# Tiny products in the left-out arms of an expert layer, an activation moved ahead, and a sum spread between blocks

## Chip, cores and metric

One core of a Trainium2 chip runs the whole kernel. The metric is the device time of one execution in microseconds (us), lower is better.

## What is computed

The reference is an encoder of two layers on 256 tokens of 1024 features. Each layer has a mixer of four branches and a feed-forward part; that of the first layer is dense, that of the second sends each token to two of eight experts. The change touches the experts alone:

```python
def moe_swiglu(x, router, w1, w3, w2):
    logits = jnp.einsum('bsd,de->bse', x, router)
    top_logit, top_idx = lax.top_k(logits, 2)
    top_w = jax.nn.softmax(top_logit, axis=-1)
    gate = jnp.sum(jax.nn.one_hot(top_idx, 8) * top_w[..., None], axis=-2)
    out = jnp.zeros_like(x)
    for e in range(8):                       # w1, w3: 1024 x 3584, w2: 3584 x 1024
        out = out + gate[..., e:e+1] * ((silu(x @ w1[e]) * (x @ w3[e])) @ w2[e])
    return out
```

All arithmetic of the experts is float32, and each expert has 42 MiB of weights.

## The kernel before

**Weights.** They come from HBM in blocks of 1 MiB (`fetch`, line 118, on SP's DMA queue), 42 for an expert: blocks 0 to 27 hold w1 and w3, 28 to 41 hold w2. They land in a ring of 21 places, and a block's load waits until the block 21 before it has been used.

**Bins.** An expert's tokens (`gather`, line 759, puts them into `xe`) stand in four bins of 32. A product takes one bin as its 32 stationary columns and streams 512 columns of weights; four such products, one for each fourth of TensorE's columns, lie beside each other in one bank of PSUM. In the profile a float32 product is two MATMUL records, so a bin of one block is 8 records. How many bins an expert needs is known only on the chip. It is loaded into TensorE's registers (`sel`), and every further bin stands in a `tc.If` (line 841) that TensorE's sequencer branches on; the other engines have no part in it.

**Stages of an expert.** `firsts(x_, q)` (line 972) runs quads q = 0, 1, 2 of eight blocks each: `quad` multiplies bin 0, then, nested, bins 1 to 3 (lines 855 to 866). Quad 3 has four blocks and takes the bins in pairs: bins 0 and 1 always, bins 2 and 3 under one `If`. `second` (line 924) does the same by pairs for the 14 blocks of w2. After a quad come `act` (silu on ScalarE, line 885, times the other half on VectorE, line 886, which reads and frees the quad's PSUM banks), `turn` (eight transposes, line 895), `turned` (copies by ScalarE and VectorE, lines 905 and 903). `where` (line 943) transposes the tokens' places. `evacuate` (hilo, lines 163 and 164) copies an expert's result out of PSUM, and `add` (lines 965 and 969) multiplies it back to the tokens, for each half t of them, with eight products on TensorE and two operations on VectorE.

**The left-out arm.** The first block of a quad must leave zeros in the banks of bins that are left out, so there the `If` has an `Else` with products of zeros, 128 stationary by 512 streamed columns in bfloat16, one for each bank (lines 858 to 860, 929). All other blocks have an `If` without an `Else`.

**Order.** Inside `tc.manual_schedule()` the order of the program is the order of each engine. An expert's w2 blocks 12 and 13 are put off until after the next expert's first quad:

```python
                        firsts(x_, 0)
                    if last:
                        seconds(last, (12, 13))
                        last.evacuate()
                    ...
                    x_.act(0)
                    ...
                    firsts(x_, 1)
                    x_.turn_places(0)
                    x_.turn(0)
                    x_.turned(0)
                    x_.act(1)
                    if last:
                        last.add()
                    x_.second_places()
                    firsts(x_, 2)
```

PSUM has four banks for the quads (`mm`), two for the second products (`s`) and two for transposes and sums (`tr`). So `firsts(x_, 1)` waits for `act(0)` to free the quad's banks, and `add`, `turn` and `where` share the two of `tr`.

Of the kernel before, what the change touches and what calls it, by code (L numbers as in the profile page):

```python
# [71 lines left out]
def trunk(tc, A, out):  # L72
    nc = tc.nc
# [573 lines left out]
    def moe(xs, gb):  # L647
        with tc.tile_pool(name="moe", bufs=1, reuse_waits="tile") as ep:
# [48 lines left out]
            zero = ep.tile([128, 512], BF16, name="zero")  # L697
# [46 lines left out]
            def places_of(e, off, oh=None, ts=(0, 1)):  # L744

                oh = ep.tile([128, 2, 128], F32, name="oh", bufs=2) if oh is None else oh
                for t in ts:
                    nc.vector.tensor_scalar(oh[:, t], iota, off + 1.0, pos[:, t, e:e + 1], op0=ALU.add, op1=ALU.is_equal)
                return oh

            def gather(oh):

                xe = ep.tile([128, 8, 128], F32, name="xe", bufs=2)
                for j in range(2):
                    ps = trp.tile([128, 4, 128], F32, name="tr")
                    for i in range(4):
                        k = 4 * j + i
                        for t in range(2):
                            nc.tensor.matmul(ps[:, i], x[t][:, k * 128:(k + 1) * 128], oh[:, t], start=t == 0, stop=t == 1)
                    if j:  # L760
                        nc.scalar.activation(xe[:, 4:8], ps, AF.Copy)
                    else:
                        nc.vector.tensor_copy(xe[:, 0:4], ps)
                return xe
# [54 lines left out]
            _, sel = nc.values_load_multi_w_load_instructions(armi[0:1, 0:NE], engines=[PE], min_val=0, max_val=3)  # L819
            over = nc.values_load(mosti[0:1, 0:1], min_val=0, max_val=S)  # L820

            class Expert:


# [9 lines left out]
                        else:  # L834
                            self.w[n] = block(self.e, n)

                def bins_over(self, n, some, none=None):

                    if self.inner:
                        return some()  # L840
                    with tc.If(sel[self.e] > n - 1) as c:  # L841
                        some()
                    if none:
                        with c.Else():
                            none()

                def quad_places(self, q):
                    self.ps[q] = [mm.tile([128, 512], F32, name="mm") for _ in range(4 if q < 3 else 2)]
# [1 line left out]
                def quad(self, q, u):  # L850

                    w, ps = self.w[8 * q + u], self.ps[q]

                    def product(k, r, g, bank, c0):
                        nc.tensor.matmul(ps[bank][32 * g:32 * g + 32], self.xe[:, k, 32 * r:32 * r + 32], w[:, c0:c0 + 512],  # L855
                                         start=k == 0, stop=k == 7)

                    def zeros(r):
                        for i in range(r, len(ps)):
                            nc.tensor.matmul(ps[i], zero[:, 0:128], zero, start=True, stop=True)  # L860

                    def bin_(r):
                        for c in range(4):
                            product(u, r, c, r, c * 512)
                        if r < 3:
                            self.bins_over(r + 1, lambda: bin_(r + 1), (lambda: zeros(r + 1)) if u == 0 else None)

                    def pair(m):
                        for kk in range(2):
                            for rr in range(2):  # L870
                                for c in range(2):
                                    product(2 * u + kk, 2 * m + rr, 2 * rr + c, m, kk * 1024 + c * 512)

                    if q < 3:
                        bin_(0)
                    else:
                        pair(0)
                        self.bins_over(2, lambda: pair(1), (lambda: zeros(1)) if u == 0 else None)

                def act(self, q):  # L880

# [29 lines left out]
                def second(self, j):  # L911

                    w, q, c = self.w[28 + j], j // 4, j % 4

                    def pair(m):
                        for i in range(2):
                            for half in range(2):
                                for rr in range(2):
                                    g = 2 * half + rr
                                    if q < 3:  # L920
                                        h = self.h[q][m][:, rr, i, 32 * c:32 * c + 32]
                                    else:
                                        h = self.h[q][0][:, m, i, 32 * (2 * rr + c):32 * (2 * rr + c) + 32]
                                    nc.tensor.matmul(self.py[m][32 * g:32 * g + 32], h,  # L924
                                                     w[:, i * D + half * 512:i * D + half * 512 + 512],
                                                     start=j == 0 and i == 0, stop=j == 13 and i == 1)

                    def zeros():
                        nc.tensor.matmul(self.py[1], zero[:, 0:128], zero, start=True, stop=True)

                    pair(0)
                    self.bins_over(2, lambda: pair(1), zeros if j == 0 else None)

                def where_places(self):
                    self.wtr = trp.tile([128, 2, 2, 128], F32, name="tr")
# [33 lines left out]
                            nc.vector.scalar_tensor_tensor(acc[t][:, c], ps[h], gate[:, t, self.e:self.e + 1], acc[t][:, c],  # L969
                                                           op0=ALU.mult, op1=ALU.add, accum_out=sums[:, t, h:h + 1])  # L970

            def firsts(x_, q):
                x_.quad_places(q)
                for u in range(8 if q < 3 else 4):
                    x_.blocks(8 * q + u)
                    x_.quad(q, u)

            def seconds(x_, js):
                for j in js:
                    x_.blocks(28 + j)  # L980
                    x_.second(j)

            with tc.manual_schedule():
                last = None
                for e in range(NE + 1):
                    x_ = None
                    if e < NE:
                        x_ = Expert(e, oh, xe)
                        firsts(x_, 0)
                    if last:  # L990
                        seconds(last, (12, 13))
                        last.evacuate()
                    if e == NE:
                        break
                    x_.act(0)
                    if e + 1 < NE:
                        oh = places_of(e + 1, 0)
                    firsts(x_, 1)
                    x_.turn_places(0)
                    x_.turn(0)  # L1000
                    x_.turned(0)
                    x_.act(1)
                    if last:
                        last.add()
                    x_.second_places()
                    firsts(x_, 2)
                    x_.turn_places(1)
                    x_.turn(1)
                    x_.turned(1)
                    x_.act(2)  # L1010
                    seconds(x_, range(4))
                    if e + 1 < NE:
                        xe = gather(oh)
                    firsts(x_, 3)
                    x_.turn_places(2)
                    x_.turn(2)
                    x_.turned(2)
                    x_.act(3)
                    seconds(x_, range(4, 8))
                    x_.turn_places(3)  # L1020
                    x_.turn(3)
                    x_.turned(3)
                    x_.where_places()
                    x_.where()
                    x_.wheres()
                    seconds(x_, range(8, 12))
                    if e == NE - 1:
                        gt = gb()
                    last = x_
                last.add(0)  # L1030

                with tc.If(over > CAP):
                    for e in range(NE):
                        oh = places_of(e, CAP)
                        x_ = Expert(e, oh, gather(oh), inner=True)
                        x_.where_places()
                        x_.where()
                        x_.wheres()
                        x_.second_places()
                        for q in range(4):  # L1040
                            firsts(x_, q)
                            x_.act(q)
                            x_.turn_places(q)
                            x_.turn(q)
                            x_.turned(q)
                            seconds(x_, range(4 * q, min(4 * q + 4, 14)))
                        x_.evacuate()
                        x_.add()
            with tc.manual_schedule():
# [6 lines left out]
                for t in range(2):  # L1056
                    for h in range(2):
                        c = norms[t].finish(h)
# [11 lines left out]
    for l in range(DEPTH):  # L1070
        xs = mixer(l, xs, lambda l=l: load_gb(1 + 2 * l))
        if l % 2 == 0:
            xs = ffn(xs, lambda: load_gb(2))
    moe(xs, lambda: load_gb(4))
    ctx.close()

# [145 lines left out]
```

## Time and profile before

| | |
|---|---|
| median of 3 runs | 1717.95 us (1715.56 to 1719.6) |
| profiled execution | 1715.06 us |
| its span in the trace | 1713.0 us |
| TensorE busy | 1580.6 us, 92% of the span |
| VectorE, ScalarE busy | 572.5 us, 426.5 us |
| experts, first product to last | 672.6 to 1695 us of the span |
| weights in the experts' part | 310 MB at up to 419 GB/s |

In the trace PE is TensorE's products, PEld its weight loads, PEq its sequencer. A timeline's row merges neighbouring records of one line: start, length, engine, line, operation, and how many; in brackets stand the idle time before it and what ended it. A length runs to the modelled end of the last record, and the next product of a stream begins a little before that, so periods are taken from start to start.

### The profile page before, as it was taken

How to read it: one execution, taken by the hardware profiler on the slowest of the kernel's cores; microseconds unless marked ns; L12 is line 12 of the kernel's file. 1: busy time of each engine (PE TensorE's matmuls, PEld its weight loads, DVE VectorE, ACT ScalarE, POOL GpSimd, SP SyncE). 2: the span in 40 equal slices, each digit the busy share in tenths (PEclk: the TensorE clock that was granted, in tenths of full speed). 3: DMA queues.
4: the chain of work that ended last, by engine and by line, in shares of the span. 5: the costliest groups of instructions: out<-in, count | busy, mean ns of one | idle time of the engine just before them, and what ended most of it. 6: DMA issues, size and time to landing. Idle time of an engine off the chain costs nothing. (4 is left out here: it accounts for less than half of the span.)

```text
span 1713.0 us, 26968 instructions
## 1 busy us (share of the span) xinstructions
PE 1580.6 (92%) x11305; PEld 820.9 (48%) x11322; DVE 572.5 (33%) x1070; ACT 426.5 (25%) x704; POOL 28.7 (2%) x29
## 2 busy tenths in 40 slices
PE   8999999999999998898899998899898899898896
PEld 7687878888868785131333332232232232232232
DVE  7688685554769674001001000100100100100102
ACT  4556644443565662010100000000010000100001
POOL 1000000000100000000000000000000000000000
PEclk9999999999999999999999999999999999999998
DMA  8345545555555547999999888778899778999700
GB/s 349 126 148 178 194 167 204 176 193 177 184 188 173 221 169 289 419 419 418 420 419 390 297 288 311 284 258 342 318 408 380 258 286 304 420 419 413 301 12 27
DMA packets 66975, 468.91 MB, mean 274 GB/s; under 512 B 7552, under 2 KB 8192, under 8 KB 11264
## 3 DMA queue, kind: packets, MB, share of 16 engines
q1 hardware_dynamic: 66816, 466.55, 71.3%
q8 instruction: 129, 2.11, 0.5%
q14 instruction: 30, 0.25, 0.0%
HBM read 465.48 MB, written 1.05 MB: 272 GB/s over the span
## 5 line engine op out<-in xcount | busy, mean ns | idle before, releaser
L855 PE MATMUL mm<-raw,xe 128*32 128x512 f32 x4416 | 519.6, 601 | 74.4 <-PEq L841 53.3
L855 PEld LDWEIGHTS mm<-raw,xe 128*32 128x32 f32 x4416 | 133.4, 110 | 430.3 <-issue 411.9
L924 PE MATMUL s<-raw,eh 128*32 128x512 f32 x2688 | 305.9, 594 | 11.5 <-PEq L841 8.7
L171 PE MATMUL mm<-w,xh 128*128 128x512 f32 (+2 forms) x1184 | 313.5, 385 | 1.9 <-ACT xh L163 1.9
L139 DVE TENSOR_TENSOR w<-raw,w 128x1024 fp32r<-128x1024 f32 (+1 forms) x198 | 238.4, 1208 | 135.2 <-ACT w L135 134.4
L135 ACT ACTIVATE w<-raw 128x1024 fp32r<-128x1024 f32 (+1 forms) x198 | 206.3, 1047 | 198.4 <-PE mm L171 172.7
L171 PEld LDWEIGHTS mm<-w,xh 128*128 128x128 f32 x1184 | 215.6, 189 | 45.5 <-ACT xh L163 3.6
L924 PEld LDWEIGHTS s<-raw,eh 128*32 128x32 f32 x2688 | 85.7, 109 | 209.4 <-issue 201.9
L171 PE MATMUL mm<-w,xl 128*128 128x512 f32 (+2 forms) x592 | 178.1, 384 | 0.7 <-DVE xl L164 0.7
L903 DVE COPY eh<-tr 128x512 f32<-128x512 f32 x24 | 16.6, 692 | 453.9 <-PE tr L895 453.9
L905 ACT ACTIVATE eh<-tr 128x512 f32<-128x512 f32 x32 | 19.1, 597 | 565.9 <-PE tr L895 565.9
L164 DVE TENSOR_TENSOR ey<-s,ey 128x512 fp32r<-128x512 f32 x16 | 10.7, 689 | 374.0 <-ACT ey L163 374.0
L171 PEld LDWEIGHTS mm<-w,xl 128*128 128x128 f32 x592 | 108.0, 189 | 22.2 <-issue 1.5
L163 ACT ACTIVATE ey<-s 128x512 fp32r<-128x512 f32 x16 | 9.1, 596 | 273.1 <-PE s L924 158.2
L520 DVE SCALAR_TENSOR_TENSOR ac<-ud,smc,ac 128x256 f32<-128x256 f32 x120 | 53.2, 479 | 0.7
L171 PE MATMUL mm<-xh,w 128*128 128x256 f32 x256 | 45.2, 289 | 0.0
L886 DVE TENSOR_TENSOR fs<-mm,fs 128x256 f32<-128x256 f32 x112 | 39.9, 415 | 15.2 <-ACT fs L885 15.1
L171 PE MATMUL mm<-w,hh 128*128 128x512 f32 x144 | 44.4, 389 | 0.0
L965 PE MATMUL tr<-ey,ohT 64*128 64x512 f32 x128 | 29.5, 480 | 13.6 <-DVE acc L969 6.7
L895 PEld LDWEIGHTS tr<-ident,fs 128*128 128x128 f32 x224 | 24.0, 141 | 34.7 <-issue 33.2
L171 PEld LDWEIGHTS mm<-xh,w 128*128 128x128 f32 x256 | 36.3, 191 | 3.2 <-issue 3.0
L885 ACT ACTIVATE fs<-mm 128x256 f32<-128x256 f32 x112 | 34.4, 399 | 13.0 <-PE mm L855 13.0
(200 smaller groups left out, 1021.0 us busy)
## 6 DMA issues: line engine op xcount, KB each, us to landing
raw<-wmoe SPq DMA_DIRECT2D x334, 1024.0 KB, 9.0
raw<-wpre SPq DMA_DIRECT2D x95, 1024.0 KB, 4.9
gb<-lnp SPq DMA_DIRECT2D x5, 1024.0 KB, 6.5
raw<-wpre SPq DMA_DIRECT2D x4, 704.0 KB, 5.9
z<-biasB SPq DMA_DIRECT2D x8, 256.0 KB, 2.7
raw<-wmoe SPq DMA_DIRECT2D x4, 512.0 KB, 7.9
z<-cw SPq DMA_DIRECT2D x2, 640.0 KB, 6.5
x<-x SPq DMA_DIRECT2D x2, 512.0 KB, 4.0
```

What stands on the lines that cost most here:

```text
L135: nc.scalar.activation(self.w[h][0], raw[:, h * self.n:(h + 1) * self.n], AF.Copy)
L139: (eng or nc.vector).tensor_tensor(wl, raw[:, h * self.n:(h + 1) * self.n], f(wh), op=ALU.subtract)
L171: nc.tensor.matmul(ps, o[i], o[j], start=start and q == 0 and k == 0, stop=stop and q == 2 and k == n - 1)
L520: later.append(lambda c=c, k=k, w=w: nc.vector.scalar_tensor_tensor(ac[:, c], ud[:, c, k:k + S], w(k), ac[:, c], op0=ALU.mult, op1=ALU.add))
L855: nc.tensor.matmul(ps[bank][32 * g:32 * g + 32], self.xe[:, k, 32 * r:32 * r + 32], w[:, c0:c0 + 512], start=k == 0, stop=k == 7)
L885: nc.scalar.activation(s, ps[:, 0:256], AF.Silu)
L886: nc.vector.tensor_tensor(s, ps[:, 256:512], s, op=ALU.mult)
L895: nc.tensor.transpose(self.tr[q][r // 2][:, r % 2, i], s[:, i * 128:(i + 1) * 128], ident)
L903: nc.vector.tensor_copy(h, tr)
L905: nc.scalar.activation(h, tr, AF.Copy)
L924: nc.tensor.matmul(self.py[m][32 * g:32 * g + 32], h, w[:, i * D + half * 512:i * D + half * 512 + 512], start=j == 0 and i == 0, stop=j = ...
L965: nc.tensor.matmul(ps[h], self.ohT[r, m, t], self.y[r, i, m], start=m == 0 and i == 0, stop=m == 1 and i == 1)
```

## The change

Three things. An `Else` arm now stands in every skip: where it held nothing, it holds `mark`, one bfloat16 product of zeros with 32 stationary columns and one streamed column, into the first bank that is left out (which holds zeros). `act(0)` of an expert stands ahead of the last expert's blocks 12 and 13 and of its `evacuate`. And `last.add()` is no longer after the second quad: its two halves stand behind blocks 3 and 6 of that quad.

```diff
+            def mark(ps):
+                nc.tensor.matmul(ps[0:32, 0:1], zero[:, 0:32], zero[:, 0:1], start=True, stop=True)
...
-                def bins_over(self, n, some, none=None):
+                def bins_over(self, n, some, none):
                     if self.inner:
                         return some()
                     with tc.If(sel[self.e] > n - 1) as c:
                         some()
-                    if none:
-                        with c.Else():
-                            none()
+                    with c.Else():
+                        none()
...
                     def zeros(r):
-                        for i in range(r, len(ps)):
-                            nc.tensor.matmul(ps[i], zero[:, 0:128], zero, start=True, stop=True)
+                        if u:
+                            mark(ps[r])
+                        else:
+                            for i in range(r, len(ps)):
+                                nc.tensor.matmul(ps[i], zero[:, 0:128], zero, start=True, stop=True)
...
-                            self.bins_over(r + 1, lambda: bin_(r + 1), (lambda: zeros(r + 1)) if u == 0 else None)
+                            self.bins_over(r + 1, lambda: bin_(r + 1), lambda: zeros(r + 1))
...
-                        self.bins_over(2, lambda: pair(1), (lambda: zeros(1)) if u == 0 else None)
+                        self.bins_over(2, lambda: pair(1), lambda: zeros(1))
...
                     def zeros():
-                        nc.tensor.matmul(self.py[1], zero[:, 0:128], zero, start=True, stop=True)
+                        if j:
+                            mark(self.py[1])
+                        else:
+                            nc.tensor.matmul(self.py[1], zero[:, 0:128], zero, start=True, stop=True)
                     pair(0)
-                    self.bins_over(2, lambda: pair(1), zeros if j == 0 else None)
+                    self.bins_over(2, lambda: pair(1), zeros)
...
-            def firsts(x_, q):
+            def firsts(x_, q, between={}):
                 x_.quad_places(q)
                 for u in range(8 if q < 3 else 4):
                     x_.blocks(8 * q + u)
                     x_.quad(q, u)
+                    if u in between:
+                        between[u]()
...
                         firsts(x_, 0)
+                        x_.act(0)
                     if last:
                         seconds(last, (12, 13))
                         last.evacuate()
                     if e == NE:
                         break
-                    x_.act(0)
                     if e + 1 < NE:
                         oh = places_of(e + 1, 0)
-                    firsts(x_, 1)
+                    firsts(x_, 1, {u: lambda t=t: last.add(t) for t, u in enumerate((3, 6))} if last else {})
                     x_.turn_places(0)
                     x_.turn(0)
                     x_.turned(0)
                     x_.act(1)
-                    if last:
-                        last.add()
                     x_.second_places()
```

## Rows read from the trace of the kernel before

**Rows 1.** Page, part 5: xcount | busy, mean ns | idle before, releasers.

```profile
L855 PE MATMUL mm<-raw,xe 128*32 128x512 f32 x4416 | 519.6, 601 | 74.4 <-PEq L841 53.3
```

**Rows 2.** Instructions of line 841: engine, operation, count, duration ns, first, last.

```profile
L841 PEldq EVENT_SEMAPHORE  x211: 51/51/51, 677.0 to 1627.9; - x106
```

**Rows 3.** DMA issues of three stretches, then busy times of one (last: GB/s).

```profile
raw<-wmoe SPq DMA_DIRECT2D x18, 1024.0 KB, 5.2
...
raw<-wmoe SPq DMA_DIRECT2D x79, 1024.0 KB, 17.0
...
raw<-wmoe SPq DMA_DIRECT2D x294, 1024.0 KB, 9.4
...
672.60:864.40 191.80, 164.24 (x1338) 50.12 (x1343) 21.07 (x57) 21.46 (x48) 0.00 (x0) 0.99 1.01 419
```

**Rows 4.** TensorE's timeline, expert 3, third quad, three bins a block.

```profile
1087.89 2.78 PE L855 MATMUL mm<-raw,xe 128*32 128x512 f32 x24
1090.93 2.78 PE L855 MATMUL mm<-raw,xe 128*32 128x512 f32 x24 [0.25 <-issue]
1094.16 2.78 PE L855 MATMUL mm<-raw,xe 128*32 128x512 f32 x24 [0.45 <-PEq L841]
```

**Rows 5.** TensorE's timeline, expert 0, first quad, two bins a block.

```profile
672.63 1.92 PE L855 MATMUL mm<-raw,xe 128*32 128x512 f32 x16
...
675.02 1.92 PE L855 MATMUL mm<-raw,xe 128*32 128x512 f32 x16
677.41 1.92 PE L855 MATMUL mm<-raw,xe 128*32 128x512 f32 x16 [0.46 <-PEq L841]
```

**Rows 6.** TensorE's timeline, expert 1, first quad, one bin a block.

```profile
773.80 1.06 PE L855 MATMUL mm<-raw,xe 128*32 128x512 f32 x8 [0.17 <-PEq L841]
...
775.55 1.06 PE L855 MATMUL mm<-raw,xe 128*32 128x512 f32 x8
...
778.03 1.06 PE L855 MATMUL mm<-raw,xe 128*32 128x512 f32 x8 [0.17 <-PEq L841]
```

**Rows 7.** TensorE's timeline, expert 0, second products, one pair a block.

```profile
735.85 1.92 PE L924 MATMUL s<-raw,eh 128*32 128x512 f32 x16 [0.25 <-issue]
...
740.05 1.93 PE L924 MATMUL s<-raw,eh 128*32 128x512 f32 x16 [0.17 <-PEq L841]
```

**Rows 8.** TensorE's timeline, expert 2, second quad, four bins, eight blocks.

```profile
898.34 27.67 PE L855 MATMUL mm<-raw,xe 128*32 128x512 f32 x256 [2.47 <-DVE fs L886]
```

**Rows 9.** TensorE's timeline, expert 0, places' transposes, then second products.

```profile
764.55 1.08 PE L943 MATMUL tr<-ident,oh 128*32 128x128 f32 x32
765.44 1.90 PE L924 MATMUL s<-raw,eh 128*32 128x512 f32 x16
```

**Rows 10.** Weight loads (PEld) in time, expert 3, third quad.

```profile
1088.78 0.13 PEld L855 LDWEIGHTS mm<-raw,xe 128*32 128x32 f32 x4 [0.30 <-issue]
```

**Rows 11.** TensorE's waits, 672 to 1694 us; all engines' timeline, expert 5.

```profile
PE mm L855 <- DVE fs L886: 9.8, 4, 2.5
...
1322.94 1.41 DVE L886 TENSOR_TENSOR fs<-mm,fs 128x256 f32<-128x256 f32 x4
...
1323.45 4.48 PE L855 MATMUL mm<-raw,xe 128*32 128x512 f32 x24 [2.47 <-DVE fs L886]
```

**Rows 12.** TensorE's timeline, expert 3, after the second quad.

```profile
1082.23 1.09 PE L895 MATMUL tr<-ident,fs 128*128 128x128 f32 x8 [0.46 <-PEq L841]
...
1086.10 0.50 PE L965 MATMUL tr<-ey,ohT 64*128 64x512 f32 x1 [0.80 <-DVE acc L969]
1086.77 1.20 PE L965 MATMUL tr<-ey,ohT 64*128 64x512 f32 x7 [0.17 <-DVE acc L969]
```

**Rows 13.** TensorE's timeline, expert 0, after the second quad.

```profile
711.21 1.09 PE L895 MATMUL tr<-ident,fs 128*128 128x128 f32 x8 [0.46 <-PEq L841]
713.46 1.06 PE L855 MATMUL mm<-raw,xe 128*32 128x512 f32 x8 [1.16 <-issue]
```

**Rows 14.** Busy times of a stretch; last: clock, DMA share, GB/s.

```profile
1480.00:1500.00 20.00, 16.68 (x99) 4.55 (x99) 4.35 (x12) 1.70 (x5) 0.00 (x0) 0.83 1.01 418
```

## The prediction

> **What bounds the kernel now.** I read the page's groups first, then the instructions of the `If` line, TensorE's timeline expert by expert, and last the loads. TensorE's products at line 855 are the costliest group, and 53.3 of the 74.4 us of idle time ahead of them were ended by TensorE's own sequencer at line 841, the `If` [rows 1]. At that line the sequencer ran 211 semaphore instructions [rows 2]. The timeline gives each expert's bins by the records of one block (8 a bin): experts 0 to 7 have 2, 1, 4, 3, 2, 3, 1 and 3. An expert has 37 skips without an `Else` (21 blocks of quads 0 to 2, three of quad 3, 13 of w2). With one or two bins all 37 are left out, with three only the 21 innermost, with four none: 4 x 37 + 3 x 21 = 211. So the count is that of the empty left-out arms, and arms that hold zeros have none. An empty arm still has to count its products as done, and does it by an instruction that waits until TensorE's products have ended. The pipeline runs dry and starts anew; the reader is to see it as the bracket of idle time in every period.
>
> Are the weights late? 18 blocks were issued before the first expert product and 79 more until 864.4, where expert 2 begins; each took 17.0 us to land at 419 GB/s, so 2.50 us a block [rows 3]. 17.0 / 2.50 = 6.8 were still on the way, so 18 + 79 - 6.8 = 90 had landed, where TensorE had used 82 (42 of expert 0, 40 of expert 1). It was 7 to 8 blocks ahead, 18 to 20 us. At the start of expert 7 it was 18 + 294 - 7 - 292 = 13 blocks, 32 us [rows 3]. TensorE's order is the bound throughout; the weights are so only if it gains over some 19 us before 864.4.
>
> **Part 1, the marks.** Four bins with no skip run at 27.67 us for 256 records, 0.865 us a bin, 0.86 without the end of the last one [rows 8]. Against that:
> three bins, empty arm: 1094.16 - 1090.93 = 3.23, less 2.58, is 0.65 [rows 4]; two bins 2.39 less 1.72 is 0.67 [rows 5]; one bin 2.48 / 2 = 1.24 less 0.86 is 0.38 [rows 6]; a pair 4.20 / 2 = 2.10 less 1.72 is 0.38 [rows 7]. The nested ones cost more, which I put down to a jump to the block's end behind the wait. So 105 arms cost 0.66 and 106 cost 0.38 us, 109.6 us in all.
>
> What replaces it shows only by neighbours. An arm with one, two and three products of zeros has a period of 3.04, 2.39 and 1.75 us [rows 4 to 6], over the bins 0.46, 0.67 and 0.89: 0.215 us for each 512 streamed columns and 0.245 fixed. The fixed part has neither the semaphore's wait nor a visible jump, but those products are 128 columns wide and want all of the array. That is the upper end for a mark, whose one column streams in nothing: **0.245**. The lower end is a change between two kinds of products that both stand 32 wide: 16 transposes of places (32 records, a quarter of the columns, so 16 / 4 x 0.86 / 4 = 0.86 us) are followed by the next stage after 0.89 [rows 9], a switch of **0.03**. Below nothing can't be, as a product is added. I take **0.08**, near the lower end, since a mark has that shape; the rest is for the one weight load behind it that can't be made early.
>
> First the row: weight loads 32 columns wide start while the products of the half before are streaming (four loads at 1088.78, in a stretch whose products are never idle) [rows 10]. [...]
>
> Gain for a nested arm 0.66 - 0.08 = 0.58, for a direct one 0.30. Experts 2 to 7: 84 nested (63 + 21), 53 direct (16 + 37): 48.7 + 15.9 = **64.6 us**. Experts 0 and 1: 21 x 0.58 + 53 x 0.30 = 28.1 us, before the cap below.
>
> **Part 2, `act(0)` ahead.** Now ScalarE and VectorE take it up after `evacuate`, and TensorE stands before quad 1 until VectorE has freed the banks: four waits of 2.4 to 2.5 us, 9.8 in all [rows 11], and three of 1.81 that the trace names "issue" (experts 3, 4, 6). VectorE's share is 1.41 us after some 0.4 on ScalarE [rows 11], and blocks 12 and 13 give at least two pair periods, 4.2 us [rows 7], of cover. So the waits go; `evacuate` slips behind, and its first user, `add`, now comes four blocks later, over 3.6 us. Both queues hold nothing else there but the next places (VectorE). No DMA is moved, so SP's queue keeps its order. Gain 2.4 us in expert 1 and **12.8** in 2 to 7.
>
> **Part 3, the sums.** From `turn` to quad 2 it is 1087.89 - 1082.23 = 5.66 us [rows 4, 12]; the seven experts with a sum give 5.65 to 6.51, 41.7 in all, 35.5 of it in 2 to 7. Without a sum it is 713.46 - 711.21 = 2.25, in which 1.16 is the wait for `act(1)` [rows 13]. So the sums now cover a wait which comes back, and that is what is late next. A sum's half that waits for nothing takes about 1087.89 - 1086.77 = 1.12 us for seven of eight products and the way back [rows 4, 12], so 1.2; two of them in the quad cost 2.4. Nothing else wants the `tr` banks there; with one bin, block 7 is short and `turn` may wait 0.2 us for VectorE. Gain in 2 to 7: 35.5 - 6 x (2.25 + 2.4) = 7.6, I take **7.3**; 1.5 in expert 1.
>
> **Part 4, the clock.** [...] Without the stalls I take it to stay up: **4.7** us in experts 4 to 6, 1.0 in expert 1. From 0 to 4.7 is open.
>
> **The cap.** Experts 0 and 1 would gain 28.1 + 2.4 + 1.5 + 1.0 = 33 us, but the loads run at their full rate there and can't come earlier: 18 to 20, **19**. From expert 2 on the loads wait for places, so they move with TensorE; expert 6 gains 37 x 0.30 and some 5 more, 16 us, of 32 at hand.
>
> **Sum.** 19 + 64.6 + 12.8 + 7.3 + 4.7 = 108.4. The profiled execution took 1715.06 us (span 1713.0), so 1606.7; the median shown lies 2.9 above it, which gives **1610**.
>
> **The rivals.**
> A, the forecast: 1610, chance 0.68.
> B, the mark is as dear as the fixed part of a zeros' arm, 0.245 (its loads and the next ones bare): experts 2 to 7 give 84 x 0.415 + 53 x 0.135 = 42, and experts 0 and 1 still reach the cap (8.7 + 7.2 + 4.9 = 21). 19 + 42 + 24.8 = 86: 1632. The two kinds of zeros' arms speak for it, rows 9 and 10 against. Chance 0.20.
> C, the moved stages give nothing: another wait comes in, above all the one for `act(1)` [rows 13] grown by a sum's operations on VectorE, and the clock falls all the same. Marks and cap alone: 84 us, 1634. Against it speaks that VectorE is idle in the quads. Chance 0.06.
> D, it doesn't do what it says: the left-out arms keep their wait, and the mark comes on top. The moves' 24.8 + 4.9 less 211 x 0.08 leave 13 us: 1705. The arms with zeros, which have no semaphore instruction [rows 2], speak against. Chance 0.03.
> E, slower: each mark empties the array in both directions and holds up the sequencer, at the skips. The arms' 109.6 and 29.7 for the moves cover 139.3 / 211 = 0.66 us a mark; beyond that point the kernel is slower, and at 0.8 it is 1747. A whole product of zeros with 512 columns has 0.46 [rows 4]. Chance 0.03.
>
> **How the numbers follow.** With the mark at 0.03 the sum gains 7 us more, and short stalls of the sequencer in expert 6 may go too: 1592 at the low end. At the high end B with half of the moves' gain: 1655; D and E are left out, 0.06, and the outer parts of A to C. A difference under 0.2% (3.4 us) can't be told from none here. Faster holds A, B, C and most of D: 0.95; same 0.02; slower 0.03.
>
> **What would show it.** Line 841 has no semaphore instructions left; three, two and one bins have periods of about 2.66, 1.80 and 0.94 us, a pair 1.80; the 2.47 and 1.81 us waits are gone; quad 2 begins 2.25 us after `turn`, with a wait for `act(1)`; late in expert 1 TensorE waits for weights, and expert 2 begins near 845; the clock holds. I would be wrong by the mark's price (periods 0.17 longer), by weights that bind elsewhere, or by sums that stall inside the quad.

## The result: 1605.45 us, and the profile after

The changed kernel takes **1605.45 us** (median, 1603.25 to 1606.61) against 1717.74 beside it: a ratio of 0.9345 [0.9329, 0.9361]. 1610 was forecast, in a range of 1592 to 1655. The spans of the two profiled executions, 1713.0 and 1604.6 us, differ by 108.4 us.

Two groups of the page after (count | busy, mean ns | idle time before them and what ended it):

```profile
L858 PE MATMUL mm<-raw,xe 128*32 128x512 f32 x4416 | 499.8, 598 | 20.2 <-issue 13.9
...
L824 PE MATMUL mm<-zero 128*32 128x1 bf16 x159 | 26.8, 168 | 8.9 <-issue 8.9
```

The branches at the `If`, before at line 841 and after at line 845 (count, least, median and longest ns, first and last start):

```profile
L841 PEldq COMPARE_BRANCH  x792: 65/174/2512, 672.5 to 1691.4; - x198
...
L845 PEldq COMPARE_BRANCH  x792: 65/176/5233, 672.7 to 1583.2; - x198
```

These answer to [rows 1, 2]. The 74.4 us of idle time ahead of the experts' products have become 20.2, the 211 semaphore instructions are gone (only the branches are left at that line, as many as before), and 211 marks stand in their place (159 into the banks of the quads, 52 into those of the second products). One number will matter: the longest branch takes 5.2 us, where it took 2.5.

The periods, in TensorE's timeline, with three bins, two bins and one bin a block:

```profile
1008.61 0.17 PE L824 MATMUL mm<-zero 128*32 128x1 bf16 x1
1008.64 3.13 PE L858 MATMUL mm<-raw,xe 128*32 128x512 f32 x24
1011.22 0.17 PE L824 MATMUL mm<-zero 128*32 128x1 bf16 x1
...
678.52 0.17 PE L824 MATMUL mm<-zero 128*32 128x1 bf16 x1
...
680.27 0.17 PE L824 MATMUL mm<-zero 128*32 128x1 bf16 x1
...
1368.88 0.17 PE L824 MATMUL mm<-zero 128*32 128x1 bf16 x1
...
1369.77 0.17 PE L824 MATMUL mm<-zero 128*32 128x1 bf16 x1
```

From mark to mark it is 2.61, 1.75 and 0.89 us, where it was 3.23, 2.39 and 1.24 [rows 4 to 6]. Over the bins (0.86 us each) that leaves **0.03 us for a mark**. The 0.17 us that each is shown as busy lies beside other products.

By expert, from its first product to that of the next one (expert 7: to the end of the span), in us; the lower lines are differences from before, those of the three runs with a part of the change alone among them:

| expert (bins) | 0 (2) | 1 (1) | 2 (4) | 3 (3) | 4 (2) | 5 (3) | 6 (1) | 7 (3) |
|---|---|---|---|---|---|---|---|---|
| before | 101.17 | 90.59 | 157.47 | 154.38 | 114.61 | 154.07 | 93.88 | 174.16 |
| after | -17.62 | +0.07 | -3.92 | -16.17 | -22.76 | -19.15 | -11.64 | -17.19 |
| marks_only | -17.95 | -0.20 | +2.11 | -13.18 | -19.72 | -12.48 | -10.55 | -12.53 |
| act_only | +0.01 | -3.33 | -2.10 | -2.02 | -3.53 | -3.82 | -5.62 | -1.04 |
| sums_only | -0.03 | -0.42 | +0.80 | -0.77 | -2.57 | -2.89 | -3.25 | -1.76 |

Expert 1 gains nothing. TensorE's waits from 672 to 1690 us (waiter, releaser: sum, times, longest) say why:

```profile
PE mm L858 <- issue: 13.9, 21, 1.4
PE mm L824 <- issue: 8.9, 6, 3.1
PE mm L858 <- DMA raw<-wmoe: 5.2, 8, 1.5
PE s L930 <- DMA raw<-wmoe: 4.6, 7, 1.6
```

The two waits for weights lie in expert 1, save two of 0.25 us each in expert 7: expert 1 is held by the loads. Expert 2 begins at 846.85 where it began at 864.39, 17.5 us earlier. The 8.9 us ahead of marks are new and lie in experts 0, 1 and 6, above all in those of one bin. TensorE's timeline in expert 6:

```profile
1403.39 1.02 PE L858 MATMUL mm<-raw,xe 128*32 128x512 f32 x5
1407.54 0.19 PE L824 MATMUL mm<-zero 128*32 128x1 bf16 x1 [3.12 <-issue]
1407.55 1.93 PE L858 MATMUL mm<-raw,xe 128*32 128x512 f32 x8
```

The window of that last block (stretch, length; busy time and count of PE, PEld, DVE, ACT, POOL; granted clock, DMA share, GB/s):

```profile
1407.55:1409.30 1.75, 1.75 (x10) 0.34 (x10) 0.00 (x0) 0.00 (x0) 0.00 (x0) 0.50 0.99 412
```

TensorE waited 3.12 us for nothing that the profile shows, and the next eight products took 1.93 us instead of 1.06 [rows 6], at a granted clock of 0.50. TensorE's sequencer had been in the branch of 5.2 us, which began at 1402.25.

From `turn` to quad 2 it is now 2.25 us, as it was where there was no sum [rows 13]:

```profile
1052.34 1.09 PE L901 MATMUL tr<-ident,fs 128*128 128x128 f32 x8
1054.59 1.92 PE L858 MATMUL mm<-raw,xe 128*32 128x512 f32 x16 [1.16 <-issue]
```

### The profile page after: what moved, and what is told of

The parts are those of the page before. It is cut to its first block, busy times and chain, and to the rows that moved or that the text cites. A ratio compares the mean times of both kernels' runs of the same rounds, so it can differ in the third digit from the quotient of the medians.

```text
span 1604.6 us, 27197 instructions
## 1 busy us (share of the span) xinstructions
PE 1539.1 (96%) x11516; PEld 861.4 (54%) x11533; DVE 574.3 (36%) x1070; ACT 427.7 (27%) x704; POOL 28.7 (2%) x29
## 3 DMA queue, kind: packets, MB, share of 16 engines
q8 instruction: 131, 2.15, 0.5%
## 5 line engine op out<-in xcount | busy, mean ns | idle before, releaser
L858 PE MATMUL mm<-raw,xe 128*32 128x512 f32 x4416 | 499.8, 598 | 20.2 <-issue 13.9
L858 PEld LDWEIGHTS mm<-raw,xe 128*32 128x32 f32 x4416 | 164.8, 110 | 267.0 <-issue 241.3
L930 PE MATMUL s<-raw,eh 128*32 128x512 f32 x2688 | 300.2, 595 | 6.3 <-DMA raw<-wmoe 4.6
L930 PEld LDWEIGHTS s<-raw,eh 128*32 128x32 f32 x2688 | 92.5, 110 | 175.9 <-issue 158.2
L824 PEld LDWEIGHTS <-zero 128*32 128x32 bf16 x211 | 20.7, 98 | 80.3 <-issue 80.3
L978 DVE SCALAR_TENSOR_TENSOR acc<-tr,egate,acc 128x512 f32<-128x512 f32 x32 | 22.8, 749 | 106.1 <-PE tr L974 106.1
L171 PE MATMUL mm<-w,yh 128*128 128x512 f32 x128 | 35.8, 401 | 0.0
L824 PE MATMUL mm<-zero 128*32 128x1 bf16 x159 | 26.8, 168 | 8.9 <-issue 8.9
```

The costliest lines, as they stand in the source:

```text
L171: nc.tensor.matmul(ps, o[i], o[j], start=start and q == 0 and k == 0, stop=stop and q == 2 and k == n - 1)
L824: nc.tensor.matmul(ps[0:32, 0:1], zero[:, 0:32], zero[:, 0:1], start=True, stop=True)
L930: nc.tensor.matmul(self.py[m][32 * g:32 * g + 32], h, w[:, i * D + half * 512:i * D + half * 512 + 512], start=j == 0 and i == 0, stop=j = ...
```

## The experiments

### One part at a time

**marks_only** is the changed kernel with `act(0)` and the sums put back:

```diff
-                        x_.act(0)
                     if last:
                         seconds(last, (12, 13))
                         last.evacuate()
...
+                    x_.act(0)
...
-                    firsts(x_, 1, {u: lambda t=t: last.add(t) for t, u in enumerate((3, 6))} if last else {})
+                    firsts(x_, 1)
...
+                    if last:
+                        last.add()
```

> The change with the marks alone; act(0) and the sums stay where they were. If each part carries its own term: the marks give 17.5 us in experts 0 and 1 (the advance at which the weights held expert 1 in the changed kernel) and 137 arms' worth in experts 2 to 7, 64.6 us at 0.08 us a mark and 71.4 us at 0.03, less about 5 us that expert 6 lost to its own sequencer. 1717.7 - 17.5 - 71.4 + 5 = 1634 us; the waits of 2.4 and 1.8 us ahead of quad 1 and the sums' 5.65 us stretches are still there. Rival (the moved stages give nothing, the marks everything): 1605 us.

Measured: 1634.63 us, 0.9526 [0.95, 0.9553], as the first theory says. Experts 2 to 7 gain 66.4 us (the table). Those with three bins, whose 21 marks are all nested, gain 13.18, 12.48 and 12.53, so 0.61 us an arm. Expert 2 has no arm to gain from and is 2.1 us longer. Its timeline at the start of quad 1 shows the wait there:

```profile
881.47 19.07 PE L858 MATMUL mm<-raw,xe 128*32 128x512 f32 x160 [2.49 <-issue]
```

And the windows ahead of that product and behind it (columns as above):

```profile
862.00:881.47 19.47, 16.98 (x163) 5.13 (x156) 1.73 (x4) 2.19 (x6) 0.00 (x0) 1.00 1.01 418
881.47:890.00 8.53, 8.53 (x64) 2.96 (x68) 1.28 (x5) 0.00 (x0) 0.00 (x0) 0.80 1.02 421
```

Behind 2.49 us of idle time the granted clock averages 0.80 for 8.5 us, in which no engine keeps TensorE waiting: 0.20 x 8.5 = 1.7 us lost to the clock.

**act_only** is the kernel before with one line moved:

```diff
                         firsts(x_, 0)
+                        x_.act(0)
...
-                    x_.act(0)
```

> The kernel before with act(0) put ahead of the last expert's evacuation and nothing else. If the term of the sum is right: the four waits of 2.4 to 2.5 us and the three of 1.81 us go, 15.2 us over experts 1 to 7: 1702.5 us, and down to 1697 if the clock also stays up behind them. Rival (another wait takes their place, for the banks of the last expert's result or in add): 1718 us, with a wait of like size before the first sum.

Measured: 1694.37 us, 0.9876 [0.9847, 0.9905], 23.0 us less, beyond the better end of what was expected. None of the 2.4 and 1.8 us waits is left. Experts 1 to 7 are 21.5 us shorter, 15.2 of it the waits; the other 6.3 came with the granted clock, which in expert 6 went from 0.96 to 1.00 (window of that expert):

```profile
1430.91:1519.17 88.26, 78.84 (x636) 24.38 (x629) 12.02 (x30) 8.75 (x22) 0.00 (x0) 1.00 1.01 414
```

**sums_only** is the kernel before with the sums behind blocks 3 and 6 of quad 1:

```diff
...
-                    firsts(x_, 1)
+                    firsts(x_, 1, {u: lambda t=t: last.add(t) for t, u in enumerate((3, 6))} if last else {})
...
-                    if last:
-                        last.add()
```

> The kernel before with the sums spread behind blocks 3 and 6 of quad 1 and nothing else. By the sum: turn to quad 2 falls from 5.65 to 6.51 to 2.25 us with a wait for act(1) of 1.16 us, two halves of 1.2 us come into the quad: 8.8 us over experts 1 to 7, 1709 us, down to 1705 with the clock's share. Rival (the halves stall in the quad as long as they did behind it): 1718 us, with idle time of TensorE behind blocks 3 and 6.

Measured: 1703.42 us, 0.992 [0.9894, 0.9945], 13.9 us less, somewhat beyond the expectation with the clock's share. `turn` to quad 2 is 2.25 us (929.11 to 931.36 in expert 2, 1.16 of it idle).

So rival C, by which the moved stages give nothing, falls. The spans of the three parts sum to 83.7 + 20.7 + 11.5 = 115.9 us, 7.5 more than together. Of that, the 3.7 us that the moves alone gain in expert 1 go to the loads, and expert 6 has 19.4 in parts and 11.6 together, for the reason found below; against that, expert 2 gains 4.7 us more together than in parts.

### What a mark costs, and why

**mark_twice** has two marks an arm, **mark_wide** one of 128 columns' width, **mark_long** one that streams 512 columns:

```diff
-                nc.tensor.matmul(ps[0:32, 0:1], zero[:, 0:32], zero[:, 0:1], start=True, stop=True)
+                for _ in range(2):
+                    nc.tensor.matmul(ps[0:32, 0:1], zero[:, 0:32], zero[:, 0:1], start=True, stop=True)
```

```diff
+                nc.tensor.matmul(ps[:, 0:1], zero[:, 0:128], zero[:, 0:1], start=True, stop=True)
```

```diff
+                nc.tensor.matmul(ps[0:32, :], zero[:, 0:32], zero, start=True, stop=True)
```

> The changed kernel with two marks in each left-out arm instead of one. If a mark costs what the periods after show, 0.03 us, and each costs that: 137 x 0.03 = 4 us in experts 2 to 7 (experts 0 and 1 are held by the weights): 1609.5 us, three bins 2.64 us. If the 0.03 is a switch paid once: 1605.5 us. Rival (a mark costs 0.245 us, its loads bare, and something else in the change gave more than its term): 137 x 0.245 = 33.6, 1639 us, three bins 2.85 us.

> The changed kernel with the mark 128 columns wide instead of 32, still one column streamed. If the 0.245 us fixed in an arm of zeros belongs to the width: 137 x (0.245 - 0.03) = 29.5 us more, 1635 us, three bins 2.82 us. Rival (it belongs to the whole bank or to the 512 columns streamed): 1605 us, three bins 2.61 us.

> The changed kernel with the mark still 32 columns wide, but 512 columns streamed into the whole bank instead of one. If a product of one column group holds up the three others as long as it streams: 137 x 0.215 = 29.5 us more, 1635 us, three bins 2.82 us. Rival (it streams beside products of the other three groups, which go on): nearer 1605 us, three bins 2.61 to 2.7 us.

Measured: 1613.07 us, 0.9393 [0.9372, 0.9413]; 1627.41 us, 0.9472 [0.9452, 0.9492]; 1627.47 us, 0.9475 [0.9455, 0.9494]. Three bins in the timeline of mark_twice:

```profile
1009.45 0.17 PE L825 MATMUL mm<-zero 128*32 128x1 bf16 x1
...
1012.09 0.17 PE L825 MATMUL mm<-zero 128*32 128x1 bf16 x1
```

of mark_wide:

```profile
1008.22 2.78 PE L858 MATMUL mm<-raw,xe 128*32 128x512 f32 x24
...
1011.04 2.78 PE L858 MATMUL mm<-raw,xe 128*32 128x512 f32 x24
```

and of mark_long:

```profile
1012.29 0.38 PE L824 MATMUL mm<-zero 128*32 128x512 bf16 x1
...
1015.08 0.38 PE L824 MATMUL mm<-zero 128*32 128x512 bf16 x1
```

The periods are 2.64, 2.82 and 2.79 us. For mark_twice the whole grows by 7.6 us (5.7 by spans, 4.9 of it in experts 2 to 7) where 4 were expected, so each mark does cost about its 0.03, and none 0.245. Over three bins (2.58) the three periods leave 0.06 us for two marks, **0.24** for a wide one and **0.21** for a long one. Both parts of the price of a whole arm of zeros, 0.245 fixed and 0.215 for 512 columns [rows 4 to 6], are found again, each by itself: the fixed part belongs to the width, the rest to the columns streamed, and a mark has neither. The expectation for mark_long takes a period of 2.8 us as a sign that one column group holds up the three others. The trace doesn't bear that out everywhere:

```profile
1012.32 2.97 PE L858 MATMUL mm<-raw,xe 128*32 128x512 f32 x24
```

Behind the mark of 1012.29 three records of the next block begin 0.03 to 0.04 us later, beside it, and the fourth after 0.22 us; so it is, within 0.1 us for the three, behind 122 of the 211 marks, while behind the other 89 all wait. In a block every column group has the same products, so one group with 0.21 us more to do could set the period alone. Which of the two it is, the period can't tell.

mark_wide and mark_long come out 8 us below what was expected, most of it in one place: expert 6 is only 1.7 and 0.4 us longer than in the changed kernel, where 37 arms at 0.21 and 0.18 us ask for 7.8 and 6.7. In expert 6 TensorE's products weren't the bound.

### Why a nested arm was dearer than a direct one

**flat_before** is the kernel before with the skips side by side, the empty arms left empty:

```diff
...
-                        if r < 3:
-                            self.bins_over(r + 1, lambda: bin_(r + 1), (lambda: zeros(r + 1)) if u == 0 else None)
...
                         bin_(0)
+                        for r in range(1, 4):
+                            self.bins_over(r, lambda: bin_(r), (lambda: zeros(r)) if u == 0 else None)
```

> The kernel before with its skips side by side instead of nested; the empty arms stay empty. It tests what was put down to a jump behind the wait, 0.28 us between a nested empty arm (0.66) and a direct one (0.38). If the nesting costs it, three bins have a period of 2.96 instead of 3.23 us, and experts 3, 5 and 7 are 21 x 0.28 = 5.9 us shorter each. If it is something else (that the products of the third bin are the ones waited for), they stay. Expert 6 now has three empty arms in a block: from nothing (TensorE has already ended) to 21 x 2 x 0.38 = 16 us more; expert 4 two of them. The whole: 1700 to 1716 by the first, 1718 to 1736 us by the second.

Measured: 1759.28 us, 1.0242 [1.0225, 1.0259]. Three bins, then one bin, in its timeline:

```profile
1061.69 2.78 PE L855 MATMUL mm<-raw,xe 128*32 128x512 f32 x24 [0.18 <-PEq L841]
1064.64 2.78 PE L855 MATMUL mm<-raw,xe 128*32 128x512 f32 x24 [0.17 <-PEq L841]
...
1477.04 1.94 PE L855 MATMUL mm<-raw,xe 128*32 128x512 f32 x8 [0.99 <-PEq L841]
1479.98 1.94 PE L855 MATMUL mm<-raw,xe 128*32 128x512 f32 x8 [1.00 <-PEq L841]
```

The window of expert 6 up to its quad 1:

```profile
1468.06:1500.73 32.67, 23.37 (x135) 4.49 (x128) 1.81 (x4) 2.30 (x6) 0.00 (x0) 0.69 0.88 338
```

Three bins have a period of 2.95 us where 2.96 was expected, and experts 3, 5 and 7 are 5.9, 6.4 and 4.5 us shorter. So the 0.28 us belong to the nesting. That it is the jump out to the block's end isn't shown: no row has the jump itself. The whole is slower than either theory has it: with one bin, three empty arms in a row idle TensorE for 1 us a block, the clock falls to 0.69, the period grows from 1.24 [rows 6] to 2.94 us, and experts 1 and 6 are 29.1 and 20.7 us longer. Expert 1 was left out of the expectation, and the clock too.

### What holds TensorE in the experts of one bin

**half_weights** loads each block by its first half and lets all products read that:

```diff
-                    ready[e, i] = fetch(src[e, i], *places[count[0] % ring], parts=2 if n >= len(order) - 2 else 1)
+                    ready[e, i] = fetch(src[e, i], *places[count[0] % ring], n=1024)
...
-                        nc.tensor.matmul(ps[bank][32 * g:32 * g + 32], self.xe[:, k, 32 * r:32 * r + 32], w[:, c0:c0 + 512],
+                        nc.tensor.matmul(ps[bank][32 * g:32 * g + 32], self.xe[:, k, 32 * r:32 * r + 32], w[:, c0 % 1024:c0 % 1024 + 512],
...
```

> The changed kernel, in which every block of the experts' weights is loaded by its first half alone and the products of the second half read the first one again; so half of the weights is left out of the computation, and the products' number and shapes stay. If the weights hold expert 1 by the bytes: its waits for blocks go, it takes 77 us instead of 90.7, and expert 2 begins near 833 instead of 846.9. Sequencer: if the branches of up to 5.2 us in expert 6 come from code that is fetched beside transfers at full rate, they shrink, and expert 6 takes 77 us instead of 82.2; the whole is 1605 - 13.7 - 5 = 1586 us. Rival (the branches are as long without that traffic): expert 6 stays at 82, 1592 us.

Measured: 1590.01 us, in one execution. The windows of experts 1 and 6:

```profile
756.15:835.08 78.93, 71.50 (x641) 26.86 (x636) 12.04 (x30) 8.64 (x22) 0.00 (x0) 0.96 0.82 282
1353.71:1431.11 77.40, 72.32 (x670) 29.19 (x666) 12.13 (x30) 8.75 (x22) 0.00 (x0) 1.00 0.81 277
```

The first theory's half is right: no wait for weights is left, expert 1 takes 78.9 us, and expert 2 begins at 835.1. **The cap in experts 0 and 1 is the weights' bytes.** On the branches it settles nothing: expert 6 does take the 77 us expected, but idle times of 3.8 us (expert 1) and 2.2 us (expert 6) are left in the run, and its longest branch (in expert 1) takes 6.1 us. The theory that they come from the transfers beside them was too simple, so two others were tried.

**flat_arms** is the kernel of the run cover (below) with the skips side by side, each with a mark:

```diff
...
-                        if r < 3:
-                            self.bins_over(r + 1, lambda: bin_(r + 1), lambda: zeros(r + 1))
...
                         bin_(0)
+                        for r in range(1, 4):
+                            self.bins_over(r, lambda: bin_(r), lambda: zeros(r))
```

> The kernel of the run called cover (1599.3 us), with the four bins of a block of quads 0 to 2 in three skips side by side, each with its own mark, and no longer one inside the other. Two theories on the stalls of TensorE's sequencer in the experts of one bin (expert 6 took 79.4 us there, 72.7 of it with TensorE busy). If a long jump is what costs, three short ones of 16 instructions each are cheaper: expert 6 takes 73 to 75 us and the whole 1595 us. If the code that is passed over has to be read whatever jumps over it, nothing is saved: expert 6 stays at 79 to 81 us, and with 63 more marks at 0.03 us the whole takes 1601 us.

Measured: 1601.85 us, 0.9322 [0.9303, 0.9341]; expert 6 takes 82.07 us. Shorter jumps save nothing.

**pad_code** adds code that only expert 2 runs:

```diff
                     def bin_(r):
+                        for _ in range(16 if r == 3 and u else 0):
+                            nc.tensor.matmul(ps[3][0:32, 0:1], zero[:, 0:32], zero[:, 0:1], start=False, stop=False)
```

> The changed kernel with 16 more products of zeros of one column, added to the bank, at the head of each innermost bin (21 blocks of quads 0 to 2), 32 instructions beside the 64 of a block's four bins. Only expert 2, with four bins, runs them: 21 x 16 x 0.03 = 10 us there. The other experts pass over them. If code that is passed over has to be read, expert 6 is longer by up to 21 x 0.89 x 32 / 64 = 9 us (82.2 to 91), and the whole takes some 1624 us; experts 3, 4, 5 and 7 stay, having more TensorE work for the same code. If only the number or the length of jumps counts (they were long before), expert 6 stays at 82 us and the whole takes 1615 us.

Measured: 1658.56 us, 0.9657 [0.9641, 0.9674]: 53 us slower than the changed kernel, for instructions that seven of the eight experts jump over. The windows of its experts 0, 3, 4 and 6:

```profile
672.83:768.88 96.05, 86.83 (x775) 32.08 (x779) 9.21 (x27) 11.82 (x25) 0.00 (x0) 0.98 1.01 419
...
1029.98:1168.17 138.19, 137.03 (x1289) 52.92 (x1285) 12.22 (x30) 8.86 (x22) 0.00 (x0) 1.00 0.87 321
1168.17:1265.73 97.56, 93.62 (x858) 34.42 (x854) 12.22 (x30) 8.86 (x22) 0.00 (x0) 1.00 1.01 410
1400.79:1496.33 95.54, 77.79 (x670) 27.84 (x665) 12.12 (x30) 8.75 (x22) 0.00 (x0) 0.95 1.01 410
```

With one bin: 13.3 us more in expert 6, 8.3 in expert 1. With two: 12.5 in expert 0, 5.7 in expert 4. With three: nothing (138.19 against 138.21). Expert 2, which runs the padding, takes 8.6 more. The expectation had the direction; it put at most 9 us on expert 6, and that two bins would be held as well it had wrong, hence 1658 and not 1624. The page's row of the queue that brings the code (packets, MB, share of 16 engines), after:

```profile
q8 instruction: 131, 2.15, 0.5%
```

and in pad_code:

```profile
q8 instruction: 152, 2.49, 0.6%
```

21 packets more, each of 2.15 MB / 131 = 16.4 KB. The padding is 21 x 32 = 672 instructions in each of eight experts, 5376 in all: 256 for each added packet. **Code that was jumped over was read like code that runs**, by these counts 256 instructions at a time. The same row for the window of expert 6 alone, after and in pad_code:

```profile
q8 instruction: 12, 0.20, 0.9%
...
q8 instruction: 15, 0.25, 1.0%
```

Expert 3, which jumps over the padding too and loses no time by it, has 13 and then 16.

That gives a balance. 13.3 us for 672 / 256 = 2.6 packets is 5.1 us for each one added, about the longest branch (5.4 us in pad_code). A block has 64 products and weight loads (256 records in eight blocks [rows 8], and as many loads), with three marks of two instructions each some 70 (an estimate from these counts, the branches left out), so by the estimate a packet covers 3.7 blocks. TensorE works on them 3.7 x 0.89 = 3.3 us with one bin, 6.4 with two and 9.5 with three. Only one bin falls short of 5.1. With the padding, some 102 instructions a block and 2.5 blocks a packet, it is 2.2, 4.4 and 6.6: one and two bins fall short, three don't, as measured. The trace's own records of queue 8 give the pace directly, and it is slower: in pad_code's experts of one and two bins the packets begin about 6 us apart (medians 5.9 to 6.2). At 6 us the balance comes out the same, with two bins just above it (6.4).

**pad_half** is pad_code with half of the weights, the edits of both:

> The run pad_code with half of the weights left out, as in half_weights (blocks loaded by their first half, the second half's products read the first again). The longer code cost expert 6 13.3 us beside weights at full rate (95.5 us against 82.2), and experts 0 and 1 12.5 and 8.3. If the instructions come late because the weights' transfers crowd out those of the code, with half the bytes expert 6 is near the 77.4 us of half_weights, at most 80, and expert 0 near 83. If code has a pace of its own, which the weights change little, expert 6 takes 88 to 95 us and expert 0 92 to 96.

Measured: 1629.2 us, in one execution. The windows of experts 0 and 6:

```profile
674.81:762.71 87.90, 82.72 (x774) 32.25 (x778) 9.20 (x27) 12.93 (x26) 0.00 (x0) 1.00 0.71 240
...
1380.34:1470.07 89.73, 77.11 (x668) 28.89 (x665) 12.12 (x30) 8.75 (x22) 0.00 (x0) 0.90 0.71 240
```

The padding costs expert 6 12.3 us over half_weights (13.3 with full traffic), expert 0 4.9 (12.5) and expert 4 1.3 (5.7). Neither theory fits alone. With two bins, close to the balance, the weights' traffic makes most of the difference, and it bears on the pace: in experts 0 and 1 packets now begin as little as 3.0 us apart, where in pad_code 5.6 was the least. With one bin an added packet still costs 12.3 / 2.6 = 4.7 us against 5.1, and the packets of expert 6 begin 6.0 us apart in the median against 6.2. The granted clock has a part in the 12.3 that wasn't taken apart: 0.90 there, 1.00 in half_weights. What sets the pace stays open.

### A version that beats both

**cover** puts a half of the sum over the wait for `act(1)`, and `turn(0)` early:

```diff
-                    firsts(x_, 1, {u: lambda t=t: last.add(t) for t, u in enumerate((3, 6))} if last else {})
-                    x_.turn_places(0)
-                    x_.turn(0)
-                    x_.turned(0)
+                    def turned_early():
+                        x_.turn_places(0)
+                        x_.turn(0)
+                        x_.turned(0)
+
+                    firsts(x_, 1, {1: turned_early, **({4: lambda: last.add(0)} if last else {})})
                     x_.act(1)
+                    if last:
+                        last.add(1)
```

> The changed kernel, with turn(0) and turned(0) behind block 1 of quad 1, the first half of the sum behind block 4, and the second half behind act(1), where TensorE waited 1.16 us for that stage in every expert. If the wait is one of cover, the second half (1.14 us of products) fills it: 6 x 1.16 = 7 us in experts 2 to 7 (expert 1 is held by the weights), 1598 us, and the wait of 1.16 us is gone. Rival (turn(0) early finds its operand late, or the second half's own way back stretches the place behind quad 1): 1605 us or up to 6 x 1.2 more, 1612 us.

Measured: **1599.34 us** (1597.78 to 1600.74), 0.9315 [0.9295, 0.9335], 6.1 us below the changed kernel in separate series whose times don't overlap (the intervals of their ratios do, by 0.0006). Experts 2 to 5 are 1.2 us shorter each, the wait of 1.16 us. In expert 3 TensorE is busy throughout; expert 6 still has 6.7 us idle, with one branch of 5.0 us (windows of both):

```profile
999.86:1136.82 136.96, 136.96 (x1289) 52.77 (x1285) 12.32 (x30) 9.08 (x22) 0.00 (x0) 1.00 0.86 323
1361.14:1440.53 79.39, 72.73 (x669) 28.05 (x665) 12.13 (x30) 8.86 (x22) 0.00 (x0) 1.00 1.00 413
```

## Why the prediction was right, step by step

The sum of 108.4 us is that of the spans to the tenth. That is partly luck: three of its terms are off and cancel.

- **What bounds it.** Right. Before, each of the 211 semaphore instructions starts 0.04 us or more behind the end of the products ahead of it: the first at 677.0 us, the products to 675.02 + 1.92 = 676.94, the next from 677.41 [rows 2, 5]. These waits left the trace with the empty arms, and rival D with them.
- **The price of a mark** was mis-sized: 0.08 us was taken, 0.03 measured, the lower bound, which the row nearest in shape had given [rows 9]. The 0.05 was the author's estimate for a weight load that can't be made early; no run shows such a load, and two marks add 0.06 us (mark_twice). So 137 x 0.05 = 6.9 us too little. The reason to stay near the lower bound holds, since mark_wide has the 0.245 of rival B and the width is what makes it. No run shows the bare loads that rival B puts by each mark: the whole mark costs 0.03 us.
- **Nested against direct.** 0.66 and 0.38 us were right, and flat_before shows that nesting makes the difference; the jump to which the prediction put it down isn't shown.
- **Expert 6** is the step that failed: "expert 6 gains 37 x 0.30 and some 5 more, 16 us". It gained 11.6; with marks at 0.03 it should have been 18. The prediction asked whether the weights could follow and not whether the instructions could. Before, the waits had slowed TensorE to 1.24 us a block, a little under the 5.1 / 3.7 = 1.4 us that a block's code takes by the estimate above; at 0.89 TensorE is well ahead of it. The hint stood in the trace of before, where the longest branch already took 2.5 us.
- **`act(0)`, the sums, the clock.** 24.8 us were forecast for experts 2 to 7; after less marks_only gives 24.7 by spans, 29.2 by medians. No run shows the 4.7 us of them that stand for the clock by themselves. Shown are, before, a first block of 4.48 us instead of 2.78 behind a wait of 2.47 [rows 4, 11] and a granted clock of 0.83 from 1480 to 1500 us [rows 14], and in act_only the 6.3 us that came with the clock. Quad 2 begins 2.25 us behind `turn`, as forecast. The split was less clean than written: alone, act_only gives 18.1 us there and sums_only 10.4 (7.3 were put on the sums). Either move alone brings part of the clock back: in expert 6 the granted clock goes from 0.96 to 1.00 with act_only and to 0.98 with sums_only, so the waits ahead of quad 1 are not alone in costing it. In expert 6 the clock didn't recover (0.96 and 0.96), as the stalls behind branches of up to 5.2 us took the place of the others.
- **The cap.** 19 was forecast, 17.5 measured; expert 2 was to begin near 845 and began at 846.9. half_weights shows that it is the weights' bytes. In that run expert 1 takes 78.9 us, with idle times of 3.8, 1.5 and 1.0 us that no wait for weights explains.

The three misses are +6.9, -6.4 (expert 6, 18 less 11.6) and -1.5 us, 1 us together.

## What to carry to other kernels

Here a skip with an empty arm cost 0.38 or 0.66 us [rows 4 to 7], and with a product 32 columns wide and one column long in its arm 0.03 (after); 128 wide it cost 0.24 (mark_wide), 512 long 0.21 (mark_long). So where an engine waits at an untaken branch, try a real instruction of the least size in the arm. Then count the code: here what was jumped over was read too (21 packets more in pad_code), and expert 6, which with one bin does the least work for the code it passes, gained 11.6 us where the marks and the moves asked for 18. A short wait that remains may be filled by moving independent products onto it, as cover does with 1.16 us an expert.

## What the runs showed of the hardware that was not expected

- 672 instructions that an expert jumps over cost it 13.3 and 8.3 us with one bin (experts 6 and 1 of pad_code), 5.7 and 12.5 with two, nothing with three. They arrive in packets of 16.4 KB, 256 instructions for each one added; with one and two bins these begin about 6 us apart (pad_code), and as little as 3.0 us with half of the weights' bytes (pad_half); single branches took up to 5.4 us with full traffic and up to 6.8 with half of it.
- A product 32 columns wide and one column long adds 0.03 us between float32 products (after), although the profile shows it as 0.17 us busy; 128 wide it adds 0.24 (mark_wide); 512 long it adds 0.21 (mark_long), though behind 122 of the 211 marks three products begin beside it.
- Three empty arms in a row in a block of 0.86 us of products lengthen its period by 2.1 us (flat_before); the granted clock, 0.69 there, has its part in that.
